# Three column blocks of parameters are issued at a later place of the list schedule

## The chip, the cores and the metric

The kernel runs on one core of one Trainium2 chip. The metric is the time of one execution on the device in microseconds (us), lower is better. TensorE is called PE below, VectorE DVE, ScalarE ACT, SyncE SP (it issues most DMAs), GpSimd POOL.

## The reference, cut to what matters

A decoder trunk of two layers on 512 tokens of width 1024. The first layer mixes tokens with a gated DeltaNet, the second with sliding window attention, and each ends in a gated MLP with a causal depthwise convolution. The change lies in the DeltaNet layer. What is computed there, and the parameters that the change touches:

```python
proj = rmsnorm(h, a_norm_w) @ a_w_in          # q, k, v, z, b, a
qkv = silu(causal_dwconv(qkv, a_conv_w))
q = l2norm(q) * 128 ** -0.5; k = l2norm(k)
o = chunked_gated_delta_rule(q, k, v, g, beta)  # chunks, triangular solve, scan
o = rmsnorm(o, a_out_norm_w) * silu(z)
h = h + o @ a_w_out
...
u = causal_dwconv(rmsnorm(h, ffn_norm_w) @ ffn_w_up, ffn_conv_w, ffn_conv_b)
h = h + (silu(gate) * val) @ ffn_w_down
...
return rmsnorm(h, final_norm_w)
```

The three blocks hold `ffn_conv_w` of both layers (128 rows of each in a block of its own, the four rows left of each in the first block), `a_out_norm_w` and `final_norm_w`. Each is first used long after the place where it is made: `a_out_norm_w` in the gating of the first finished heads, the convolution weights in the first MLP, the last norm at the very end.

## The kernel before, in words

**Dense products.** Every projection is computed in tiles of 128 output columns by 512 tokens. A float32 product is split into three passes (`mm3`: high by high, low by high, high by low), so one tile of a projection from 1024 inputs is 24 PE instructions of shape 128x512, called dense products here (lines L162, L163, L164). They collect in one of three PSUM banks with the tag "d". The weights arrive by SP in stages of 256 columns (`load_stage`, two buffers), and `cast` splits them on ACT (L132) and DVE (L133).

**What follows a tile.** `conv_silu` reads the bank: one ACT step (L277), three DVE steps (L280) and a silu on ACT (L281). It works in a row with the tag "acc" (two buffers) and writes, for values, a row "va" (two buffers). A bank "d" is free once the three DVE steps are done.

**Heads in four groups.** For each group of heads the words of `ORDER` name jobs: K and Q, key and query projections; V, value projections; B, key norms (`key_norms`, L433 to L455); P, key products (`key_products`, L464 to L482, with exponentials on ACT, L475); T, A and R, turned keys (L519), query products (L508, L511) and query norms (L500); I, a triangular solve on DVE (62 short steps, L555 and L561); L, block steps that finish the inverse (`levels`, L585 to L615); C, the scan over four chunks (L635 to L682); z and g, the gate projections and the gating of a finished head. Nearly all of the short PE steps collect in one of only two banks with the tag "g", which ACT or DVE must empty before the next but one step can write.

**What sets the order.** The program is written as one sequence, and a list scheduler puts the instructions of each engine into a fixed order by priority and by when it expects operands and buffers. Each job gets a priority by its place: `base + 1000 * (100 + pos + SHIFT[letter])`, a lower number first. B has a shift of -28, so the key norms come early although their word stands second; V2 and V3 of the first group stand at 118 and 119. What is written before the loop, like the columns, has an earlier priority than all jobs. At run time an engine works its row strictly in order. The buffers of a tag, on the other hand, are handed out in the order in which the program is written.

**Columns.** `columns` loads rows of parameters into a row (for the three blocks the tag "f", by SP), turns them on PE with the identity (L235) into a bank "g", and copies the bank to a constant on DVE (L237). Before the change the three blocks are written after the gates of the DeltaNet and ahead of the loop over `ORDER`.

Of the kernel before, what the change touches and what calls it, by code (L numbers as in the profile page):

```python
# [17 lines left out]
P = 128  # L18
# [17 lines left out]
]  # L36

SHIFT = {"R": 6, "B": -28, "g": -40, "K": -1, "N": 7, "C": -2, "P": -3}


@with_exitstack
def kernel(
# [64 lines left out]
    def row(tag, dt=F32, n=T):  # L107
        return main.tile([P, n], dt, tag=tag, bufs=ROWS[tag], name=nm(tag))
# [4 lines left out]
    def bank(tag):  # L113
        return psum.tile([P, T], F32, tag=tag, bufs=BANKS[tag], name=nm(tag))

    def const(shape, dt=F32, s="c"):
        return cp.tile(list(shape), dt, name=nm(s))
# [109 lines left out]
    def columns(parts, n, s, q=SP, tag="acc", place="g"):  # L227
        st = row(tag, n=P)
        r = 0
        for ap in parts:  # L230
            k = ap.shape[0]
            q.dma_start(st[r : r + k, :], ap)
            r += k
        ps = bank(place)
        PE.transpose(ps[:, :n], st[:n, :], ident[:n, :n])  # L235
        t = const([P, n], s=s)
        V.tensor_copy(t[:], ps[:, :n])  # L237
        return t
# [16 lines left out]
    for c in range(NC):  # L255
        junk = main.tile([P, D], F32, tag="nt", bufs=2, name=nm("junk"))
        r = const([P, 1], s="rx")
# [5 lines left out]
    for k in range(KD):  # L263
# [3 lines left out]
        h, l = row("xh", F32R), row("xl", F32R)  # L267
# [68 lines left out]
    for c in range(NC):  # L336
# [25 lines left out]
        base=0,  # L362
# [13 lines left out]
    def hc(ap):  # L376
# [32 lines left out]
    zd = dp.tile([HV, P, T], F32, name="zd")  # L409
    yd = dp.tile([HV, P, T], F32, name="yd")  # L410

    fconv_rows = ffn_conv_w.rearrange("l j (r c) -> l (j r) c", c=P)
    onw_c = columns(
        [
            fconv_rows[0, 128:132, :],
            fconv_rows[1, 128:132, :],
            a_out_norm_w,
            final_norm_w.rearrange("(r c) -> r c", c=P),
        ],
        17,  # L420
        "onwc",
        tag="f",
    )
    fcw = [columns([fconv_rows[l, 0:128, :]], 128, "fcw", tag="f") for l in range(2)]

    def key_norms(g):
        pr = slice(2 * g, 2 * g + 2)
        st[g]["kk"] = pair("m32")
        for i in range(2):
            kT = st[g]["k"][:, i, :]  # L430
            ps = bank("g")
            cut = [slice(c * P, (c + 1) * P) for c in range(NC)]
            together([lambda cs=cs: PE.matmul(ps[:, cs], kT[:, cs], kT[:, cs], start=True, stop=True) for cs in cut])  # L433
            S.copy(st[g]["kk"][:, i, :], ps[:])
            diag = row("va")
            d3 = diag[:].rearrange("p (c t) -> p c t", c=NC)
            V.tensor_tensor(
                d3,
                ps[:].rearrange("p (c t) -> p c t", c=NC),
                ident[:].unsqueeze(1).to_broadcast([P, NC, P]),  # L440
                op=ALU.mult,
            )
            V.tensor_reduce(sse[:, 0, 2 * g + i, :], d3, axis=AX.X, op=ALU.add)
        V.tensor_scalar(sse[:, 0, pr, :], sse[:, 0, pr, :], EPS, None, op0=ALU.add)
        V.reciprocal(rk2[:, pr, :], sse[:, 0, pr, :])
        S.activation(nk[:, pr, :], sse[:, 0, pr, :], AF.Sqrt)
        for i in range(2):
            hs = slice(4 * g + 2 * i, 4 * g + 2 * i + 2)
            V.tensor_tensor(
                brk[:, hs, :],  # L450
                beta_t[:, hs, :],
                rk2[:, 2 * g + i : 2 * g + i + 1, :].to_broadcast([P, 2, NC]),
                op=ALU.mult,
            )
            V.tensor_tensor(kap[:, hs, :], brk[:, hs, :], egd[:, hs, :], op=ALU.mult)  # L455
# [308 lines left out]
    heads = {"z": 0, "g": 0}  # L764
    base = tc.cur_priority
    pos = 0
    for i, line in enumerate(ORDER):
        for word in line.split():
            a, n = word[0], [int(d) for d in word[1:]]
            pos += 1  # L770
            target = base + 1000 * (100 + pos + SHIFT.get(a, 0))
            with tc.high_priority(tc.cur_priority - target):
                if a in heads:
                    (gate_proj if a == "z" else gate)(heads[a])
                    heads[a] += 1
                elif a.isupper():
                    JOBS[a](i, *n)
                else:
                    JOBS[a.upper()](i - 1, *n)
# [664 lines left out]
```

## Time and profile before

| | |
|---|---|
| time, median of 3 runs | 1415.96 us (1414.63 to 1419.01) |
| span of the profiled execution | 1412.6 us; its own time beyond the span is not recorded |
| PE, PEld, DVE, ACT busy | 98%, 83%, 78%, 53% of the span |
| granted PE clock | 0.999 over the span |
| DeltaNet layer up to its last scan and gates | about the first 450 us |
| three column transposes on PE | 42.6 to 45.9 us |
| first key norms on PE | 46.9 us |
| first `levels` of group 0 on PE | 126.6 us |

The page lists the busy time of each engine and the costliest groups of instructions; the view of the waits says for each instruction what ended the idle time ahead of it; the timeline lists instructions by start and duration, merged where equal ones follow each other (a number after x counts them). PE instructions overlap, so that a dense product that lasts 0.39 us is followed by the next after some 0.23 us. A float32 product appears twice or more in the timeline's count for one row of the program.

### The profile page before, as it was taken

What the parts mean: (1) busy time and instruction counts of PE and PEld (TensorE: products, weight loads), DVE (VectorE), ACT (ScalarE), POOL (GpSimd) and SP (SyncE); (2) the same over time, 40 slices, a digit from 0 to 9 for tenths busy, and PEclk for the clock granted to TensorE, in tenths of its full rate; (3) what the DMA queues carried; (4) which work ended last, traced back from release to release, by engine and by line L of the source; (5) the groups of instructions that cost most, each with busy time, mean ns of one, the idle gap of its engine ahead of it and who ended that gap; (6) DMA issues with size and microseconds to landing.
All of it is one profiled execution on the core that took longest, in us unless ns stands there. A gap on an engine that the chain in (4) does not pass through costs nothing.

```text
span 1412.6 us, 21751 instructions
## 1 busy us (share of the span) xinstructions
PE 1384.7 (98%) x8370; PEld 1167.1 (83%) x8370; DVE 1108.1 (78%) x2070; ACT 748.1 (53%) x1470; POOL 15.6 (1%) x37
## 2 busy tenths in 40 slices
PE   7999999999999999999999999999999999999998
PEld 5787888878877888888988889777788888988897
DVE  4996896978856438879878889788668888878996
ACT  7764566656658225444344446567544444444543
POOL 1000000000100000000000000000000000000000
PEclk9999999999999999999999999999999999999999
DMA  5333254172465323221443223322132231432222
GB/s 161 92 103 115 79 175 126 61 231 84 140 225 159 119 90 112 90 90 46 135 150 119 75 79 109 109 71 76 61 112 90 90 101 49 146 106 82 92 75 75
DMA packets 162299, 151.80 MB, mean 107 GB/s; under 512 B 24148, under 2 KB 150677, under 8 KB 162197
## 3 DMA queue, kind: packets, MB, share of 16 engines
q1 hardware_dynamic: 159938, 150.22, 33.2%
q8 instruction: 66, 1.08, 0.3%
q10 hardware_dynamic: 2259, 0.20, 0.1%
q14 instruction: 36, 0.29, 0.1%
HBM read 133.60 MB, written 15.75 MB: 106 GB/s over the span
## 4 chain that ended last, share of the span: by engine, by line
PE 87%; DVE 6%; DMA 2%; ACT 2%; issue 1%; SPq 0%; DVEq 0%; ACTq 0%
PE d L162 20%; PE d L163 20%; PE d L164 20%; PE g L198 2%; DVE wlo L133 2%; PE d L1054 1%; PE d L1207 1%; PE d L1211 1%; PE d L1209 1%; PE d L1052 1%; PE d L1053 1%; PE s L1054 1%; PE s L1052 1%; PE s L1053 1%; PE s L659 1%
## 5 line engine op out<-in xcount | busy, mean ns | idle before, releaser
L162 PE MATMUL d<-xh,whi 128*128 128x512 f32 x1128 | 444.2, 394 | 0.2
L163 PE MATMUL d<-xl,whi 128*128 128x512 f32 x1128 | 444.0, 394 | 0.0
L164 PE MATMUL d<-xh,wlo 128*128 128x512 f32 x1128 | 441.9, 393 | 0.3 <-DVE wlo L156 0.3
L132 ACT CAST whi<-stage 128x1024 fp32r<-128x1024 f32 (+2 forms) x234 | 227.4, 976 | 247.7 <-PE d L163 165.1
L133 DVE TENSOR_TENSOR wlo<-stage,whi 128x1024 fp32r<-128x1024 f32 (+2 forms) x234 | 263.4, 1128 | 70.4 <-ACT whi L132 69.6
L162 PEld LDWEIGHTS d<-xh,whi 128*128 128x128 f32 x1128 | 211.7, 188 | 44.9 <-ACT xh L172 0.5
L164 PEld LDWEIGHTS d<-xh,wlo 128*128 128x128 f32 x1128 | 211.6, 188 | 44.6 <-DVE wlo L156 0.7
L163 PEld LDWEIGHTS d<-xl,whi 128*128 128x128 f32 x1128 | 211.7, 188 | 43.2 <-issue 0.5
L280 DVE SCALAR_TENSOR_TENSOR acc<-d,cwc,acc 128x511 f32<-128x511 f32 (+2 forms) x96 | 70.7, 739 | 8.7 <-ACT acc L277 7.9
L913 DVE TENSOR_TENSOR sz<-d,p6s 128x512 f32<-128x512 f32 x59 | 40.6, 688 | 42.9 <-PE d L164 40.7
L935 ACT ACTIVATE dt<-dt 128x512 f32<-128x512 f32 x44 | 27.8, 631 | 78.3 <-DVE dt L918 78.3
L918 DVE SCALAR_TENSOR_TENSOR dt<-sz,fcw,dt 128x511 f32<-128x511 f32 (+1 forms) x60 | 44.8, 747 | 1.8 <-ACT dt L916 0.9
L918 DVE SCALAR_TENSOR_TENSOR va<-sz,fcw,va 128x511 f32<-128x511 f32 (+1 forms) x58 | 43.3, 747 | 0.9
L561 DVE TENSOR_TENSOR sT<-sT,p6s 64x31 f32<-64x31 f32 (+15 forms) x124 | 40.9, 330 | 2.0
L555 DVE TENSOR_TENSOR p6s<-sN,sT 64x31 f32<-64x31 f32 (+15 forms) x124 | 40.7, 328 | 1.9
L1276 ACT ACTIVATE dt<-dt,sm 128x256 f32<-128x256 f32 (+1 forms) x64 | 30.1, 471 | 21.5 <-DVE sm L1259 21.5
L132 ACT CAST whi<-st 128x768 fp32r<-128x768 f32 (+1 forms) x30 | 23.7, 792 | 30.5 <-PE g L1053 9.0
L913 DVE TENSOR_TENSOR zl<-d,p6s 128x512 f32<-128x512 f32 x29 | 20.0, 688 | 17.8 <-PE d L164 17.8
L682 ACT ACTIVATE rq<-o 128x128 f32<-128x128 f32 x64 | 19.0, 301 | 25.4 <-DVE o L677 22.3
L937 DVE TENSOR_TENSOR va<-dt,va 128x512 f32<-128x512 f32 x44 | 30.4, 690 | 1.2
L133 DVE TENSOR_TENSOR wlo<-st,whi 128x768 fp32r<-128x768 f32 (+1 forms) x30 | 26.8, 899 | 2.2 <-ACT whi L132 2.2
L916 ACT ACTIVATE dt<-sz,normc,fcw 128x512 f32<-128x512 f32 x30 | 24.5, 815 | 6.5 <-DVE sz L913 6.0
(770 smaller groups left out, 2876.2 us busy)
## 6 DMA issues: line engine op xcount, KB each, us to landing
stage<-in_ffn_w_up_dram SPq DMA_DIRECT2D x44, 1024.0 KB, 4.8
stage<-in_a_w_in_dram SPq DMA_DIRECT2D x23, 1024.0 KB, 5.8
stage<-in_ffn_w_down_dram SPq DMA_DIRECT2D x16, 768.0 KB, 4.3
stage<-in_a_w_out_dram SPq DMA_DIRECT2D x8, 1024.0 KB, 5.0
st<-in_ffn_w_down_dram SPq DMA_DIRECT2D x8, 768.0 KB, 5.3
zd<-sz SPq DMA_DIRECT2D x16, 256.0 KB, 2.6
od<-o SPq DMA_DIRECT2D x16, 256.0 KB
stage<-in_b_w_q_dram SPq DMA_DIRECT2D x4, 1024.0 KB, 5.0
```

The lines of the kernel that those rows point to most:

```text
L132: S.copy(hi[:, :kt, :m], src)
L133: V.tensor_tensor(lo[:, :kt, :m], src, hi[:, :kt, :m].bitcast(F32), op=ALU.subtract)
L162: PE.matmul(ps, hi[:, k, :m], xh[k], start=first and k == 0, stop=False)
L163: PE.matmul(ps, hi[:, k, :m], xl[k][:], start=False, stop=False)
L164: done.append(PE.matmul(ps, lo[:, k, :m], xh[k], start=False, stop=last and k == kt - 1))
L280: V.scalar_tensor_tensor(acc[:, d:], ps[:, : T - d], col, acc[:, d:], op0=ALU.mult, op1=ALU.add)
L555: V.tensor_tensor(tv, N[:, s, s + 1 : 32].unsqueeze(2).to_broadcast([64, n, m]), Tm[:, s : s + 1, 0:m].to_broadcast([64, n, m]), op=ALU.mult,)
L561: V.tensor_tensor(Tm[:, s + 1 : 32, 0:m], Tm[:, s + 1 : 32, 0:m], tv, op=ALU.subtract)
L913: V.tensor_tensor(u[:], ps[:], rs[:], op=ALU.mult)
L918: V.scalar_tensor_tensor(acc[:, d:], u[:, : T - d], tap(2 - d, t), acc[:, d:], op0=ALU.mult, op1=ALU.add)
L937: V.tensor_tensor(b[:], a[:], b[:], op=ALU.mult)
L1276: S.activation(ej, ej, AF.Exp, bias=ngm[:, i : i + 1], scale=-1.0, accum_out=den[:, i : i + 1])
```

## The change

The code that makes the three blocks moves behind the definitions of all jobs, directly ahead of the loop over `ORDER`, and gets a priority of its own, that of a job at place 20: behind V2 and V3 of the first group (118 and 119), and ahead of most of the second line of `ORDER`. Nothing else changes; the same DMAs, transposes and copies are issued.

```diff
+COLUMNS = 20
 SHIFT = {"R": 6, "B": -28, "g": -40, "K": -1, "N": 7, "C": -2, "P": -3}
...
-    fconv_rows = ffn_conv_w.rearrange("l j (r c) -> l (j r) c", c=P)
-    onw_c = columns(
...
-    fcw = [columns([fconv_rows[l, 0:128, :]], 128, "fcw", tag="f") for l in range(2)]
...
     base = tc.cur_priority
     pos = 0
+    with tc.high_priority(tc.cur_priority - base - 1000 * (100 + COLUMNS)):
+        fconv_rows = ffn_conv_w.rearrange("l j (r c) -> l (j r) c", c=P)
+        onw_c = columns(
+            [
+                fconv_rows[0, 128:132, :],
+                fconv_rows[1, 128:132, :],
+                a_out_norm_w,
+                final_norm_w.rearrange("(r c) -> r c", c=P),
+            ],
+            17,
+            "onwc",
+            tag="f",
+        )
+        fcw = [columns([fconv_rows[l, 0:128, :]], 128, "fcw", tag="f") for l in range(2)]
     for i, line in enumerate(ORDER):
```

The line numbers of the changed program are one higher up to the old place of the block and 13 lower between the two places (L433 becomes L420, L464 becomes L451, L508 becomes L495, L605 becomes L592). The numbers at the end of names tell buffers apart in the order of the program.

**First place, PE, the columns and the first key norms, before.** These rows follow the turned gates; the names are g_365, g_371, g_377 for the columns and g_420 for the first key norms, and d_634 is the first query tile.

```order
L235 MATMUL g_365<-ident_81,f_360 128x17
L162 MATMUL d_634<-xh_178,whi_635 128x512
L163 MATMUL d_634<-xl_179,whi_635 128x512
L164 MATMUL d_634<-xh_178,wlo_636 128x512
L162 MATMUL d_634<-xh_187,whi_635 128x512
L235 MATMUL g_371<-ident_81,f_369 128x128
L235 MATMUL g_377<-ident_81,f_375 128x128
L163 MATMUL d_634<-xl_188,whi_635 128x512
L164 MATMUL d_634<-xh_187,wlo_636 128x512
L162 MATMUL d_634<-xh_196,whi_635 128x512
L163 MATMUL d_634<-xl_197,whi_635 128x512
L433 MATMUL g_420<-kT_206 128x128 x4
```

The same place in the changed program. Here d_843 is the tile of the value head V3, and d_1186 the first key tile of the second group of heads.

```order
L165 MATMUL d_843<-xh_196,wlo_845 128x512
L236 MATMUL g_368<-ident_81,f_363 128x17
L236 MATMUL g_374<-ident_81,f_372 128x128
L163 MATMUL d_1186<-xh_133,whi_1187 128x512
L236 MATMUL g_380<-ident_81,f_378 128x128
L164 MATMUL d_1186<-xl_134,whi_1187 128x512
L420 MATMUL g_420<-kT_206 128x128 x4
L420 MATMUL g_429<-kT_206 128x128 x4
L165 MATMUL d_1186<-xh_133,wlo_1188 128x512
```

Counted along PE's row, 87 dense products stand ahead of the first column transpose before, and 192 in the changed program. The key norms have moved with the columns, from behind 95 dense products to behind 194: they stand after the columns in both, and their banks are numbered after those of the columns.

**Second place, PE, the short steps of the first group.** Before, they are spread between dense products; around the first value transpose (g_579) and the first turned keys (g_623) PE's row reads as follows, where d_721 is the tile of V1.

```order
L162 MATMUL d_721<-xh_178,whi_722 128x512
L198 MATMUL g_579<-ident_81,va_540 128x128 x4
L198 MATMUL g_623<-ident_81,kT_206 128x128 x4
L163 MATMUL d_721<-xl_179,whi_722 128x512
L164 MATMUL d_721<-xh_178,wlo_723 128x512
```

In the changed program the third and fourth key product (g_475, g_489), the value transposes of V0 and V1 (from va_540, va_720), the turned keys, two query products and two query transposes stand in one piece.

```order
L451 MATMUL g_475<-gr_301,skr_315 128x512
L452 MATMUL g_475<-mnegr_322,identr_86 128x512
L451 MATMUL g_489<-gr_301,skr_315 128x512
L452 MATMUL g_489<-mnegr_322,identr_86 128x512
L199 MATMUL g_579<-ident_81,va_540 128x128 x4
L199 MATMUL g_623<-ident_81,kT_206 128x128 x4
L495 MATMUL g_704<-qT_631,kT_206 128x128 x4
L495 MATMUL g_712<-qT_631,kT_206 128x128 x4
L199 MATMUL g_756<-ident_81,va_720 128x128 x4
L199 MATMUL g_765<-ident_81,qT_631 128x128 x4
L199 MATMUL g_775<-ident_81,qT_631 128x128 x4
L199 MATMUL g_786<-ident_81,kT_206 128x128 x4
```

Ahead of this piece lies dense product 216, the last of d_1186, and behind it comes d_1221; between the two no dense product is left. ACT's row for the same stretch in the changed program (dt are the exponentials of the key products, nk the root of the key norms, va the silu of V0 and V1):

```order
L462 ACT_TABLE_LOAD
L462 ACTIVATE dt_449<-g_446,ngc_331 128x128
L433 ACT_TABLE_LOAD
L433 ACTIVATE nk_351<-sse_350 128x8
L462 ACT_TABLE_LOAD
L462 ACTIVATE dt_449<-g_446,ngc_331 128x128 x3
L462 ACTIVATE dt_463<-g_460,ngc_331 128x128 x4
L462 ACTIVATE dt_478<-g_475,ngc_331 128x128 x4
L462 ACTIVATE dt_492<-g_489,ngc_331 128x128 x4
L282 ACT_TABLE_LOAD
L282 ACTIVATE va_540<-acc_572 128x512
L282 ACTIVATE va_720<-acc_750 128x512
```

Before, too, the table loads and the 16 exponentials stand ahead of the silu of V0 on ACT; what has moved is that PE now has its row of short steps, and no dense product, beside them.

**Third place, PE, the end of the fourth group's `levels`.** Before, dense products of the last gate projection (d_4404) stand between its steps; p_4050 and s_4061 are its last two block steps, s_4133 is the first product of the scan.

```order
L162 MATMUL d_4404<-xh_160,whi_4405 128x512
L163 MATMUL d_4404<-xl_161,whi_4405 128x512
L164 MATMUL d_4404<-xh_160,wlo_4406 128x512
L605 MATMUL p_4050<-Xg,nt_3418 64x64 x8
L162 MATMUL d_4404<-xh_169,whi_4405 128x512
L163 MATMUL d_4404<-xl_170,whi_4405 128x512
L164 MATMUL d_4404<-xh_169,wlo_4406 128x512
L612 MATMUL s_4061<-sy_4001,p6s_347 64x64 x8
L651 MATMUL s_4133<-vt_3773,sy_3929 128x128 x2
```

In the changed program, where d_4625 and d_4683 are the first tiles of the output projection:

```order
L581 MATMUL s_4022<-sy_4001,pz_346 32x32
L592 MATMUL p_4050<-Xg,nt_3418 64x64 x8
L599 MATMUL s_4061<-sy_4001,p6s_347 64x64 x8
L638 MATMUL s_4133<-vt_3773,sy_3929 128x128 x2
L163 MATMUL d_4625<-kT_4478,whi_4626 128x512
L163 MATMUL d_4683<-kT_4478,whi_4684 128x512
L638 MATMUL s_4133<-vt_3866,sy_4001 128x128 x2
```

All 1152 dense products of the layer's input projections are issued ahead of these steps now. From the first half's middle step (s_3950) to s_4133, 17 dense products stand between the steps before, and none now. In the scan behind, four dense products stand now between the second chunk's two pieces (L638 and L646), where none stood before (L651 and L659), and one instead of four between the same pieces of the first chunk.

More of the change, by code (lines that the diff above doesn't have):

```diff
@@ L410 @@
     yd = dp.tile([HV, P, T], F32, name="yd")
-    fconv_rows = ffn_conv_w.rearrange("l j (r c) -> l (j r) c", c=P)
-    onw_c = columns(
[L414 to L423, printed above, removed]
-    fcw = [columns([fconv_rows[l, 0:128, :]], 128, "fcw", tag="f") for l in range(2)]
     def key_norms(g):
```

## The prediction

> **What bounds the kernel now.** I read the page's busy times first, then the waits of PE up to 520 us, then the timeline where the change works.
>
> ```profile
> span 1412.6 us, 21751 instructions
> PE 1384.7 (98%) x8370; PEld 1167.1 (83%) x8370; DVE 1108.1 (78%) x2070; ACT 748.1 (53%) x1470; POOL 15.6 (1%) x37
> ```
>
> PE is busy for 98% of the span, so a wait of PE that comes or goes moves the end by its length, unless a later one absorbs it. How much there is to win the waits tell (engine, line, what it waited for: us in total, times, longest):
>
> ```profile
> PE g L235 <- DMA xt<-in_x_dram: 8.4, 1, 8.4
> PE g L235 <- DVE onwc L237: 1.7, 1, 1.7
> PE p L659 <- ACT us L653: 1.5, 1, 1.5
> PE g L198 <- ACT ol L720: 1.0, 1, 1.0
> PE s L266 <- DVE xt L261: 0.7, 1, 0.7
> PE d L162 <- ACT kT L168: 0.5, 1, 0.5
> ```
>
> Behind the start-up there are four waits in 520 us, 4.7 us together. One belongs to the columns. The next rows give it and the pace of the dense products:
>
> ```profile
> 27.89 0.40 PE L162 MATMUL d<-xh,whi 128*128 128x512 f32 x1
> ...
> 42.00 0.39 PE L164 MATMUL d<-xh,wlo 128*128 128x512 f32 x1
> 42.23 0.44 PE L370 MATMUL g<-ident,sz 80*128 80x80 f32 x4
> ...
> 45.41 0.17 DVE L237 COPY onwc<-g 128x17 f32<-128x17 f32 x1
> ...
> 45.63 0.48 PE L235 MATMUL g<-ident,f 128*128 128x128 f32 x2 [1.68 <-DVE onwc L237]
> ```
>
> From 27.89 to 42.00 lie 63 dense products: (42.00 - 27.89) / 62 = 0.2276 us each. The second column transpose needs the bank of the first, whose copy waited in DVE's queue until 45.41.
>
> **The change, step by step.** No work is added or removed; PE's row is permuted, and the question is what PE waits for in the new row. I write T for the time since PE reaches the first column transpose there.
>
> *The old wait goes: -1.7.* At the new place DVE stands empty before the copies, since the last convolution ahead of them belongs to the tile V1, two tiles back. Three copies of the kind above then cost PE some 0.3 us. T = 0 lies at 42.7 + 105 x 0.2276 = 66.6 us, 105 dense products behind the turned gates. Until there nothing should wait: a tile takes 24 x 0.2276 = 5.5 us of PE and, by the next rows, about 3 x 0.73 + 1.21 = 3.4 us of DVE.
>
> *The new piece without dense products.* The key norms did not pass the columns but were pulled back with them, behind 99 more dense products. V0 to V3 cannot finish before them: two hold the two rows "acc", and V2, V3 and the next key tile fill the three banks "d". So PE runs out of dense products at number 216, and works the piece of ten short groups alone. The rows that price it:
>
> ```profile
> 43.62 1.21 DVE L133 TENSOR_TENSOR wlo<-stage,whi 128x1024 fp32r<-128x1024 f32 x1
> ...
> 46.88 2.00 PE L433 MATMUL g<-kT 128*128 128x128 f32 x16
> 48.03 0.59 ACT L434 COPY m<-g 128x512 f32<-128x512 f32 x1 [0.32 <-PE g L433]
> 48.65 0.69 DVE L437 TENSOR_TENSOR va<-g,ident 128x512 f32<-128x512 f32 x1 [0.43 <-ACT m L434]
> 49.49 0.46 PE L464 MATMUL g<-gr,skr 128*128 128x512 f32 x1
> ...
> 53.23 1.28 ACT L446 ACT_TABLE_LOAD   x1
> ...
> 56.03 2.18 ACT L475 ACTIVATE dt<-g,ngc 128x128 f32<-128x128 f32 x8
> 58.22 1.28 ACT L281 ACT_TABLE_LOAD   x1
> 59.52 0.63 ACT L281 ACTIVATE va<-acc 128x512 f32<-128x512 f32 x1
> 60.22 0.64 PE L198 MATMUL g<-ident,va 128*128 128x128 f32 x4
> ...
> 61.15 1.14 ACT L538 ACTIVATE vt<-g,nk 128x128 f32<-128x128 f32 x4
> ...
> 61.94 1.28 DVE L519 TENSOR_TENSOR ktok<-g,kap 128x512 f32<-128x512 f32 x2
> ...
> 63.14 2.89 DVE L280 SCALAR_TENSOR_TENSOR acc<-d,cwc,acc 128x510 f32<-128x510 f32 x4
> 63.24 0.69 ACT L277 ACTIVATE acc<-d,cwc 128x512 f32<-128x512 f32 x1
> ...
> 66.39 1.95 PE L508 MATMUL g<-qT,kT 128*128 128x128 f32 x16
> ...
> 67.73 2.47 DVE L511 TENSOR_TENSOR at<-g,dt 128x512 f32<-128x512 f32 x4
> ...
> 70.12 0.17 DVE L555 TENSOR_TENSOR p6s<-sN,sT 64x31 f32<-64x31 f32 x1
> ...
> 77.67 0.27 ACT L500 ACTIVATE va<-g 128x128 f32<-128x128 f32 x1
> ```
>
> PE reaches the piece at T = 9.4: 24 dense products 5.5, columns 0.6, key norms 2.0, two key products 0.6 each. ACT meanwhile: the norms start at T = 1.2, the second copy (0.59, from 48.03) is over at 3.8; then a table load 1.28, one exponential 0.27, a load, the root 0.2, a load, and the other seven exponentials 1.9: T = 10.2, when the fourth key product gets its bank. PE ends it at 10.9. Then eight exponentials 2.2, a load 1.3 and the silu 0.63 end at 14.3 on ACT; the transpose of V0 needs it, so PE is idle for 3.5. The turned keys follow to 15.3. A query product needs the bank of V0, which ACT empties (1.14) behind a second silu and a convolution step (1.2): 16.7, idle 1.4. Two query products (1.95) end at 18.6. V1's transpose waits for the first of them to be read: DVE does ktok (1.28), two convolution steps (1.45) and two of the four at (1.24) by 19.5, idle 0.9; the first query transpose waits for the other two, 20.8, idle 0.8; the second for ACT's copies of V1, 0.1; the last turned keys for four squares with their sums (about 1.2 from 77.67 on), 22.6, idle 0.8. PE leaves the piece at T = 23.0. Of these 13.6 us its own work is 1.3 + 0.9 + 1.95 + 1.8 = 5.9. **Wait: 7.7.** Behind it two value transposes and the next key norms wait some 0.2 to 0.3 each for silus that come late: with the columns' 0.3, **0.9**.
>
> Bounds: at least the 3.5 for V0 and half of the rest, 5.5, were the chain behind it to overlap better than I draw it; at most 11, with 0.4 more at each of eight hand-overs (the end of the silu at 60.15 to 60.22 in the rows shows 0.1).
>
> [...]
>
> *Group 0 comes later: 0, between 0 and 3.* Its solve starts on DVE (70.12 now) at about T = 25.7, 92.3 us. Its `levels` stand behind 419 dense products instead of 385, at 66.6 + 23.0 + 203 x 0.2276 + about 7 for short steps = 142.8. So 50.5 us are left between them, where now it is 56.4:
>
> ```profile
> 126.55 0.24 PE L585 MATMUL s<-Xg,nt 32*32 32x32 f32 x2
> ```
>
> Yet DVE has three convolution steps and two weight splits less in between (3 x 0.73 + 2 x 1.21 = 4.6), so I take nothing. The 16 DMAs of the key products wait on SP behind two weight stages more; these load before the products exist. If the cover is gone, PE waits 1 to 3 us here.
>
> *The end of the layer: +2.1.* The 17 dense products between the fourth group's `levels` steps are gone, and its chain through DVE and ACT stays:
>
> ```profile
> 405.38 0.50 PE L162 MATMUL d<-xh,whi 128*128 128x512 f32 x1
> 405.51 0.42 DVE L596 TENSOR_SCALAR Xg<-s 32x256 f32<-32x256 f32 x1 [1.36 <-PE s L594]
> 406.28 0.68 PE L605 MATMUL p<-Xg,nt 64*64 64x64 f32 x16
> ...
> 407.06 0.76 ACT L608 COPY p6s<-p 64x256 f32<-64x256 f32 x2 [2.58 <-PE p L605]
> 407.78 0.76 PE L612 MATMUL s<-sy,p6s 64*64 64x64 f32 x16
> ```
>
> Each step starts 0.1 to 0.4 behind the one it needs, so the chain is no shorter without the dense products, and PE waits for their 17 x 0.2276 = 3.9. In the scan the 1.5 (L659) and 0.5 (L162) of the waits go, as four dense products stand there now; the first chunk's copy (0.6 with 0.3 of hand-over) has one dense product instead of four and costs 0.65. Now three dense products from 405.38 end at 406.06 and the next step starts at 406.28, so 0.2 is waited for already; I take the same for the other half. Sum 3.9 + 0.65 - 1.5 - 0.5 - 0.4 = 2.1. Bounds -2 (nothing of the 3.9 seen) and +5.
>
> **Sum:** -1.7 + 7.7 + 0.9 + 0 + 2.1 = +9.0. The profiled span of 1412.6 becomes 1421.6. The three timed runs lie 2.0 to 6.4 above that span, the median 3.4; I add the sum to the median: 1416.0 + 9.0 = 1425.0.
>
> **Rivals.** *The wait is hidden.* The piece is fed faster than I draw, the layer's end loses nothing, and only the columns' wait goes: 1416.0 - 1.7 = 1414.3. For it: now PE passes the same steps without a wait. Against: now 93 dense products stand among these ten groups (between numbers 106 and 199), and then none.
>
> *Faster.* Convolutions and casts run ahead by 24 us, and the scan's end finds its operands ready: 1.7 + 1.5 + 0.5 + 1.0 (L198) = 4.7 go, 1411.3. This decides only if the ten groups wait under 1 us in all, while two banks and the exponentials already demand 3.5 for V0 alone.
>
> *A slower PE clock.* The array was slower after its idle start:
>
> ```profile
> 13.54 0.80 PE L162 MATMUL d<-xh,whi 128*128 128x512 f32 x1
> ...
> 19.95 0.39 PE L164 MATMUL d<-xh,wlo 128*128 128x512 f32 x1
> ```
>
> The same product took 0.80 and later 0.39. If the 13.6 us of thin work bring this back, the 5.9 us in them double at most, of which about half lies on the chain, and the dense products behind lose 1 to 2: +4, 1429. [...] Late `levels` of group 0 (+1 to +3) end in the same place.
>
> *The change does what it says,* with the columns behind the key products: 1414.3 as well. The key norms' banks are numbered behind the columns', and their rows stand behind them, so it has no chance of its own.
>
> **How the numbers follow.** Forecast 1425, own range 1420.3 to 1428, chance 0.55. Slower clock or late `levels`, about 1429, 0.25. Wait hidden, about 1414 to 1420, 0.17. Faster, 0.03. A measurement of this kernel can tell about 0.3%, 4.2 us, from no change: slower 0.80, same 0.17, faster 0.03. The range takes in the low bound of the piece with a gain at the end (-1.7 + 5.5 + 0.3 - 2 = +2) and the high one (-1.7 + 11 + 0.9 + 5 = +15): 1417.5 to 1431.
>
> **What the profile would show.** Right: no wait at L236 above 0.5; the key norms near 68 us; PE waiting 6 to 9 us between about 76 and 90, first 3 to 4 us for ACT's silu of V0, then for DVE's at and ACT's squares; waits of 3 to 4 us in the fourth group's `levels`. Wrong: waits under 3 us in the piece, a first `levels` of group 0 that waits, or dense products of 0.8 behind it.

## The result, and the profile after

| | before | after |
|---|---|---|
| time, median of 6 runs each, taken together | 1417.78 us (1414.63 to 1419.52) | 1429.88 us (1428.56 to 1432.95) |
| ratio to before, 95% interval | | 1.0094 (1.0080 to 1.0107) |
| profiled execution: time, span | not recorded, 1412.6 us | 1429.34 us, 1427.5 us |
| granted PE clock over the span | 0.999 | 0.994 |

The change makes the kernel slower by 12.1 us (the difference of the medians). The forecast was 9.0 us and a time of 1425.0; of the 4.9 us between this and 1429.88, 1.8 is the base, whose median moved from 1415.96 to 1417.78 with three more runs. The two profiles are executions with a clock at the upper end of what their kernels show: 0.999, where the 61 executions of the kernel before in the sets of the experiments have 0.995 to 0.999, and 0.994, where the change's other five have 0.992 and 0.993. Line numbers of the changed kernel are used from here on: L163 to L165 dense products, L199 turns, L236 columns, L420 key norms, L451 and L452 key products, L495 query products, L579 to L599 `levels`, L638 and L646 the scan.

The page's head and its busy times, after:

```profile
span 1427.5 us, 21769 instructions
PE 1391.6 (97%) x8370; PEld 1171.3 (82%) x8370; DVE 1109.5 (78%) x2070; ACT 748.9 (52%) x1471; POOL 12.6 (1%) x37
```

PE executes the same 8370 instructions and is busy 6.9 us longer. So only about half of the 14.9 us that the span grew is idle time; the rest is slower work. The waits of PE up to 490 us (instruction, what it waited for, us in total, times, longest; the first is the start-up, and smaller ones follow):

```profile
PE g L236 <- DMA acc<-in_ffn_conv_b_dram: 7.8, 1, 7.8
PE g L199 <- ACT va L282: 3.3, 1, 3.3
PE g L199 <- ACT ol L707: 1.4, 3, 0.7
PE p L592 <- DVE Xg L583: 1.1, 2, 0.5
PE g L199 <- DVE at L498: 1.0, 1, 1.0
PE s L599 <- ACT p6s L595: 1.0, 2, 0.5
PE d L163 <- ACT at L169: 0.9, 1, 0.9
PE s L579 <- ACT pz L575: 0.8, 1, 0.8
PE g L199 <- ACT va L487: 0.8, 1, 0.8
...
```

The columns' wait of 1.7 is gone. V0's turn waits 3.3 for its silu, the forecast's largest single wait. Waits of about 0.5 stand ahead of the fourth group's `levels` steps. The timeline of PE in the early stretch (start, us, line, tiles, shape, count, idle before it and what ended it):

```profile
65.85 2.02 PE L420 MATMUL g<-kT 128*128 128x128 f32 x16
...
78.95 1.12 PE L199 MATMUL g<-ident,va 128*128 128x128 f32 x4 [3.29 <-ACT va L282]
79.86 1.06 PE L199 MATMUL g<-ident,kT 128*128 128x128 f32 x4
81.30 3.77 PE L495 MATMUL g<-qT,kT 128*128 128x128 f32 x16 [0.38 <-ACT vt L525]
84.90 0.63 PE L199 MATMUL g<-ident,va 128*128 128x128 f32 x4
86.54 1.06 PE L199 MATMUL g<-ident,qT 128*128 128x128 f32 x8 [1.00 <-DVE at L498]
88.40 0.66 PE L199 MATMUL g<-ident,kT 128*128 128x128 f32 x4 [0.79 <-ACT va L487]
88.81 0.48 PE L163 MATMUL d<-xh,whi 128*128 128x512 f32 x1
```

The key norms stand at 65.85, 19 us later than before. Behind the long wait the same turn takes 1.12 and then, at 84.90, 0.63, and the query products take 3.77 where they took 1.95 before. The view by stretches says why (us, busy PE, PEld, DVE, ACT and POOL with their instructions, granted clock, DMA share, GB/s). Before, in two windows, one of each stretch:

```profile
80.00:85.00 5.00, 5.00 (x27) 4.10 (x27) 4.90 (x14) 3.44 (x12) 0.00 (x0) 1.00 0.05 17
405.00:410.00 5.00, 5.00 (x93) 3.94 (x83) 2.64 (x6) 1.87 (x4) 0.30 (x1) 1.00 0.54 172
```

After:

```profile
80.00:85.00 5.00, 4.62 (x22) 4.13 (x21) 3.80 (x6) 2.65 (x6) 0.00 (x0) 0.51 0.17 26
85.00:90.00 5.00, 3.20 (x22) 2.46 (x22) 4.82 (x9) 3.94 (x22) 0.00 (x0) 1.00 0.17 56
420.00:425.00 5.00, 3.96 (x43) 3.45 (x38) 4.30 (x8) 2.49 (x5) 0.30 (x1) 0.50 0.38 129
```

The clock was halved in the early stretch (0.51) and again at the layer's end (0.50), where in the profile of before it was 1.00 in every such window. The second pair of the last `levels` steps, after:

```profile
420.62 1.12 PE L592 MATMUL p<-Xg,nt 64*64 64x64 f32 x16 [0.52 <-DVE Xg L583]
422.26 1.50 PE L599 MATMUL s<-sy,p6s 64*64 64x64 f32 x16 [0.52 <-ACT p6s L595]
423.69 1.22 PE L638 MATMUL s<-vt,sy 128*128 128x128 f32 x4
```

The same steps took 0.68 and 0.76 before. **To count both losses** I read windows of 1 us from 36 to 490 us, and take as idle the part in which PE isn't busy, and as slow its busy part times (1 - clock). Two of these rows, after:

```profile
79.00:80.00 1.00, 1.00 (x5) 1.00 (x6) 0.05 (x1) 0.99 (x2) 0.00 (x0) 0.50 0.22 34
420.00:421.00 1.00, 0.48 (x13) 0.38 (x8) 0.82 (x2) 1.00 (x2) 0.00 (x0) 0.50 0.21 70
```

The first adds 0.50 to slow and nothing to idle, the second 0.24 to slow and 0.52 to idle. The sums of 454 rows:

| us, idle / slow | 36-60 | 60-110 | 110-400 | 400-440 | 440-490 | all |
|---|---|---|---|---|---|---|
| before | 1.67 / 0 | 0.04 / 0 | 1.18 / 0 | 1.99 / 0 | 0.09 / 0 | 4.97 / 0 |
| after | 0 / 0 | 5.75 / 2.79 | 2.03 / 0 | 3.77 / 2.81 | 1.24 / 0 | 12.79 / 5.60 |

That is 7.8 more idle and 5.6 slow, 13.4 together, beside 14.9 in the spans and 12.1 in the medians. The 0 of slow before holds for the profiled execution alone: of those 61 executions, the 13 with a clock of 0.999 took 1415.2 on average and the 9 with 0.996 took 1419.6, so most executions of the kernel before lose some time to the clock too, at a place that no kept trace shows.

Last, the stores of the four groups' solves (line, count, ns, first and last start), before, and then after:

```profile
L564 SPq DMA_DIRECT2D td<-sT x4: 471/494/655, 119.4 to 381.0; - x4
```

```profile
L551 SPq DMA_DIRECT2D td<-sT x4: 474/492/498, 132.6 to 396.2; - x4
```

The first solve ends 13.2 later and the fourth 15.2 later: the lateness of the key norms is handed from group to group. PE's dense products are late by less (by 8.0 at the 1151st, counted with the gates' 24: 406.96 instead of 398.94), and in PE's fixed row all of them stand ahead of the fourth group's last `levels` steps now.

### The profile page after: what moved, and what is told of

The parts are those of the page before. It is cut to its first block, busy times and chain, and to the rows that moved or that the text cites. A ratio compares the mean times of both kernels' runs of the same rounds, so it can differ in the third digit from the quotient of the medians.

```text
span 1427.5 us, 21769 instructions
## 1 busy us (share of the span) xinstructions
PE 1391.6 (97%) x8370; PEld 1171.3 (82%) x8370; DVE 1109.5 (78%) x2070; ACT 748.9 (52%) x1471; POOL 12.6 (1%) x37
## 4 chain that ended last, share of the span: by engine, by line
PE 85%; DVE 6%; DMA 4%; ACT 3%; issue 1%; DVEq 0%; SPq 0%; ACTq 0%
PE d L163 19%; PE d L165 19%; PE d L164 19%; PE g L199 2%; DVE wlo L134 2%; DMA ol<-od 1%; PE d L1208 1%; PE d L1212 1%; PE d L1210 1%; PE d L1055 1%; PE s L638 1%; PE d L1053 1%; PE d L1054 1%; PE s L1055 1%; PE s L646 1%
## 5 line engine op out<-in xcount | busy, mean ns | idle before, releaser
L165 PE MATMUL d<-xh,wlo 128*128 128x512 f32 x1128 | 444.3, 395 | 1.2 <-DVE wlo L134 0.9
L163 PE MATMUL d<-xh,whi 128*128 128x512 f32 x1128 | 444.3, 394 | 0.2
L165 PEld LDWEIGHTS d<-xh,wlo 128*128 128x128 f32 x1128 | 211.6, 188 | 46.4 <-DVE wlo L134 1.9
L163 PEld LDWEIGHTS d<-xh,whi 128*128 128x128 f32 x1128 | 211.8, 188 | 44.1 <-issue 0.6
```

Of the source, the lines that this page charges most:

```text
L163: PE.matmul(ps, hi[:, k, :m], xh[k], start=first and k == 0, stop=False)
L165: done.append(PE.matmul(ps, lo[:, k, :m], xh[k], start=False, stop=last and k == kt - 1))
```

## The experiments

Each kernel is compared with the kernel before, run in the same set on the same chip. The column "all" is the sum of idle and slow of that kernel's profile, and of the work without use that it adds, less the 4.97 of before; the last column is the difference of the medians in its set.

| run | median us | ratio, 95% interval | idle | slow | added | all | medians |
|---|---|---|---|---|---|---|---|
| 1 other banks | 1419.04 | 1.0013 (1.0000 to 1.0027) | 6.80 | 1.71 | | +3.5 | +2.2 |
| 2 one late | 1431.51 | 1.0095 (1.0077 to 1.0113) | 13.49 | 5.77 | | +14.3 | +14.7 |
| 3 norms late alone | 1431.87 | 1.0100 (1.0078 to 1.0122) | 15.07 | 5.63 | | +15.7 | +15.2 |
| 4 COLUMNS 16 | 1427.43 | 1.0065 (1.0048 to 1.0083) | 11.98 | 5.81 | | +12.8 | +10.6 |
| 5 end alone | 1424.52 | 1.0062 (1.0041 to 1.0082) | 7.63 | 6.88 | | +9.5 | +8.7 |
| 6 end undone | 1441.05 | 1.0168 (1.0146 to 1.0189) | 16.16 | 15.30 | | +26.5 | +25.2 |
| 7 early filled | 1429.35 | 1.0080 (1.0063 to 1.0097) | 10.06 | 4.42 | 3.2 | +12.7 | +12.5 |
| 8 end filled, first try | 1433.96 | 1.0124 (1.0105 to 1.0143) | 11.63 | 7.52 | 1.8 | +16.0 | +18.2 |
| 9 end filled, half width | 1432.04 | 1.0102 (1.0085 to 1.0118) | 10.61 | 7.71 | 2.6 | +16.0 | +15.4 |
| 10 both, half width at the end | 1432.40 | 1.0110 (1.0094 to 1.0125) | 8.17 | 6.65 | 5.8 | +15.7 | +15.8 |
| 11 end filled, full width | 1427.30 | 1.0071 (1.0056 to 1.0086) | 9.33 | 2.49 | 3.6 | +10.5 | +9.2 |
| 12 both, full width | 1426.74 | 1.0069 (1.0049 to 1.0090) | 8.38 | 3.41 | 6.8 | +13.6 | +9.4 |
| 13 norms five products later | 1417.97 | 1.0012 (0.9996 to 1.0028) | 6.10 | 0 | | +1.1 | +2.2 |

The two last columns agree within 2.3 us in every row but the twelfth, from 1 to 26 us. The sums are those of one execution each, the medians of 4 to 17. So what a version costs is read on PE, as waits plus slow clock.

### What holds the work back: runs 1 to 3

**1, other banks.** The late transposes write to another tag:

```diff
-            tag="f",
-        )
-        fcw = [columns([fconv_rows[l, 0:128, :]], 128, "fcw", tag="f") for l in range(2)]
+            tag="f",
+            place="s",
+        )
+        fcw = [columns([fconv_rows[l, 0:128, :]], 128, "fcw", tag="f", place="s") for l in range(2)]
```

> The three late transposes write to the two PSUM banks of tag s instead of the two of tag g; nothing else differs from the change. The transposes then still stand behind dense product 192, but the key norms stand behind 87, as before, and the ten short groups have dense products among them again; the layer's end has the order of before. Theory A (what costs is the order in which tag g hands out its banks: it holds back the key norms and empties two stretches of dense products): no wait of PE over 1.0 us between 75 and 95, granted clock 1.00 in the 5 us windows from 75 to 90 and from 415 to 430, and a time of 1416 (1414 to 1418), at or 1.7 under the kernel before. Rival B (the late place of the transposes, their copies and their loads costs by itself): a time within 2 us of the change, 1428 to 1432.

Measured 1419.04, 2.2 over the kernel before (interval 0 to 0.27%), and no wait or slow clock between 60 and 110. Rival B (1428 to 1432) falls. Theory A has the mechanism; the time is 1 us above its range, and in the profile another wait stands in the place of the columns' wait. PE of this kernel:

```profile
43.84 0.47 PE L163 MATMUL d<-xh,whi 128*128 128x512 f32 x1
46.23 1.18 PE L420 MATMUL g<-kT 128*128 128x128 f32 x8 [1.92 <-ACT gt L375]
47.15 0.70 PE L164 MATMUL d<-xl,whi 128*128 128x512 f32 x1
47.64 0.63 PE L165 MATMUL d<-xh,wlo 128*128 128x512 f32 x1
...
50.62 0.41 PE L163 MATMUL d<-xh,whi 128*128 128x512 f32 x1
```

The second key norms need the bank of the turned gates and wait 1.92 for ACT's copy of it. Behind that, dense products start 0.43 apart instead of 0.23 up to 50.6: the clock was halved here too (0.50 in every half microsecond from 47.5 to 50.5).

**2, one late.** Only the second `fcw` gets the later place, the rest stands as before.

```diff
+    fcw = [columns([fconv_rows[0, 0:128, :]], 128, "fcw", tag="f")]
...
+        fcw.append(columns([fconv_rows[1, 0:128, :]], 128, "fcw", tag="f"))
```

> Only the second block of 128 rows (the second fcw) has the later place; the other two stand where they stood before. Theory A: a single late block holds back the bank as three do; PE's order between dense products 192 and 216 and in the layer's end is that of the change, so 1430 (1428 to 1432), with two clock windows near 0.5. Rival B (the cost goes with the number of late blocks): a third of the 12 us, 1422 (1420 to 1424).

Measured 1431.51, as theory A has it. The cost does not go with the number of late blocks: one in the ring of tag g is enough.

**3, norms late alone.** The kernel before, its columns at their old place, with one tie:

```diff
+    behind(st[0]["norms", 0], passes[HQK * P + 256][0])
```

> The kernel before with its three blocks of columns at their old place, and one tie: the first group's first key norms stand behind the first dense products of the second group's key projection (number 195). PE's order from there on, the piece of ten short groups and the layer's end, is that of the change. Theory A (what costs is the key norms that are held back; the columns are only what holds them in the change): as the change and a columns' wait of 1.7 more, 1431.5 (1429 to 1433.5), clock 0.5 for some microseconds near 80 and near 420. Rival B (the late columns, their loads and copies cost a part): under 1427.

Measured 1431.87, at theory A's 1431.5, with the columns' wait back (1.82 idle from 36 to 60) and the clock down in both stretches (0.50 in the half microseconds from 81.5 to 84.5, 0.50 from 420 to 425). With run 1 this settles who is to blame: late columns with early key norms cost 2.2, early columns with late key norms 15.2.

### The two stretches apart: runs 4 to 6

**4, COLUMNS 16.**

```diff
-COLUMNS = 20
+COLUMNS = 16
```

> COLUMNS is 16 instead of 20: the transposes stand behind dense product 144, the key norms behind 146, and the ten short groups have dense products among them up to number 211; the layer's end has the order of the change, with all 1152 dense products of the projections issued before the fourth group's last levels steps. Theory A (two drained stretches with costs of their own, +7.3 early and +5.9 at the layer's end): the early stretch costs -1.7 to +1.5, the layer's end +5.9 again, about +1 behind it, so 1424 (1421 to 1427); clock 1.00 from 75 to 90 and about 0.5 from 420 to 425. Rival B (the loss at the layer's end follows from the late early stretch): clock 1.00 at the layer's end and a time of 1417 to 1420.

Measured 1427.43, just above theory A's range, and rival B (1417 to 1420) falls: from 60 to 110 PE idles 0.4 and the clock stays (1.00 in the three windows of 5 us from 75 to 90), and the layer's end still idles 3.4 and loses 4.1. What theory A missed is the middle, 5.0 idle and 1.7 slow from 110 to 400, the first of it here:

```profile
135.78 0.22 PE L572 MATMUL s<-Xg,nt 32*32 32x32 f32 x2 [0.68 <-DMA Xg<-td]
137.15 0.87 PE L199 MATMUL g<-ident,va 128*128 128x128 f32 x4 [1.16 <-ACT va L282]
```

Here the first `levels` of group 0 waits for its solve. Its solves' stores, the view of the result's last two fences:

```profile
L551 SPq DMA_DIRECT2D td<-sT x4: 471/492/499, 126.8 to 393.9; - x4
```

They are late too (7.4 and 12.9 us), though PE lost nothing early. Time that PE does not lose early it loses where the late solves are needed.

**5, end alone.** The kernel before, with one tie that puts the fourth group's first step behind the projections' last dense product:

```diff
+    behind(st[3]["step"][0], passes[QKV + 256 * 7 + P][-1])
```

> The kernel before, its columns at their old place, with one tie added: the fourth group's first levels step with pz stands behind the last dense product of the projections, as in the change. Nothing of the early stretch differs from before. Theory A: the layer's end alone costs +5.9 over the kernel before, 1422.7 (1421 to 1424.5), with clock 0.5 for some 6 us between 410 and 430 and waits of about 0.5 at each step. Rival B (the loss needs the early delay too): 1416 to 1418.5.

Measured 1424.52, at the upper end of theory A's range: the emptied layer's end costs 8.7 on its own. It is no exact copy of the change's end. The clock was low for 17.1 us (407.5 to 424.6) instead of 6.8, and one wait in it is longer:

```profile
409.47 0.47 PE L614 MATMUL s<-sy,p6s 64*64 64x64 f32 x2 [3.21 <-ACT p6s L609]
```

ACT made that copy only at 409.05, behind a weight cast that waited for its DMA until 407.98. The bound is therefore rough.

**6, end undone.** The change, its last 24 dense products of the projections tied behind the steps:

```diff
+BEHIND = (7, 15, 15, 23, 31, 31, 39, 39)
...
+    s3 = st[3]["step"]
+    for k, at in enumerate(BEHIND):
+        behind(starts[QKV + 256 * 7 + P][k], s3[at])
```

> The change, with the last 24 dense products of the projections tied behind the fourth group's levels steps, three to a step at most places, so that the layer's end has dense products among its steps as the kernel before has; the early stretch, with its ten short groups in one piece, stays as the change has it. Theory A (the layer's end costs +5.9, because its steps lost the dense products that covered their waits and kept the clock up): clock 1.00 from 415 to 430, still 0.5 in 80 to 85, and a time of 1424 (1422.5 to 1425.5). Rival B (the layer's end is late for another reason, its loads or ACT's and DVE's work): 1428 to 1431, with the waits at other instructions.

A miss: 1441.05, beyond both. The moved products were missing ahead of the steps, where they had covered ACT's and DVE's work (waits of 1.97 at 412.75 for ACT's `ol` and 1.96 at 416.90 for DVE's `sy`), the clock fell at 413.8, and did not come back for 24 us:

```profile
425.00:430.00 5.00, 5.00 (x56) 2.96 (x55) 2.12 (x4) 1.06 (x2) 0.00 (x0) 0.50 0.50 157
430.00:435.00 5.00, 5.00 (x41) 3.90 (x41) 1.20 (x3) 0.73 (x2) 0.30 (x1) 0.50 0.01 3
```

In this order group 0's first `levels` also waited for its solve (2.1 at L580), and 1.6 were lost to the clock there, as in run 4. So this order does not give the cover back: what is put between the steps is missing ahead of them. That the steps lost their cover stays the reading of the trace and of run 5, not of this run.

### What the clock costs: runs 7 to 12

All of these are the change with products without use (the mask by the identity) added to keep the array working. **7** puts 14 ahead of V0's transposes:

```diff
+            if (g, hh) == (0, 3):
+                fill = bank("p")
+                st[0]["fill"] = [
+                    PE.matmul(
+                        fill[:].rearrange("p (c t) -> p c t", c=NC),
+                        identr[:],
+                        mnegr[:].unsqueeze(1).to_broadcast([P, NC, P]),
...
+                    for _ in range(FILL)
+                ]
+                behind(st[0]["fill"][0], bias)
```

> The change, plus 14 products of 128x512 without use (the mask by the identity, into the bank of tag p that nothing reads then) between the last key product of the first group and V0's transposes, 14 x 0.2276 = 3.2 us of work in the 3.3 us in which PE waits for silu of V0. Everything else stands in the same order. Theory A (the 3.3 us of idle lower the clock, and the lower clock lies on PE's path through the short groups): clock 1.00 from 75 to 90, the 16 query products 1.95 instead of 3.77, dense products resume 1.5 to 3 us earlier, time 1427.5 (1426 to 1428.5). Rival C (the short groups are fed by ACT and DVE, and PE's clock there is hidden): clock 1.00, but longer waits in place of the slower products, and a time of 1429 to 1431.

The clock stayed, 1.00:

```profile
80.00:85.00 5.00, 3.06 (x25) 2.55 (x23) 4.46 (x8) 2.99 (x7) 0.00 (x0) 1.00 0.18 29
```

The query products took 2.05, but the waits behind them grew (1.03, 0.91, 0.56 and 0.54 at the four that follow), and the median is 1429.35, rival C's. Counted at the 311th dense product of each trace, less the offset at the 7th (the start differs by up to 2 us between runs), the change is 7.3 later than before and this kernel 6.2. The other profiles in which the early stretch is as the change has it give 7.1 to 7.3 (runs 6, 8, 9 and 11), the one of run 12, where the clock stayed as well, 6.1, and that of run 10, where it fell in spite of the added work, 7.1. Of the early loss about 1.1 is the clock; the rest of the 2.8 is hidden behind ACT and DVE. The median does not show the 1.1, since it holds the layer's end as well, where this profile lost 4.4 to the clock and that of the change 2.8.

**8** puts four products of 128x256 behind each of four steps at the layer's end, into the bank that the step has written:

```diff
+FILLED = ((3, 0, 3), (3, 0, 6), (3, 0, 7), (3, 1, 1))
...
+        def fill(ps, step):
+            for _ in range(KEEP if (g, pr, step) in FILLED else 0):
...
+        fill(p3, 3)
```

> The change, plus 16 products of 128x256 without use (four into the unused half of each of four banks of the fourth group's levels steps), 16 x 0.114 = 1.8 us of work, in waits of PE of about 0.5 each. Theory A (of the +5.9 at the layer's end some 3.4 is the lower clock and 2.5 waits): clock 1.00 from 415 to 430, the steps back at their lengths of before (0.76 instead of 1.50), time 1427 (1425.5 to 1428.5). Rival C (as in the early stretch, where a full clock took 1.1 off 7.3, the waits grow by what the steps shrink): clock 1.00 and a time of 1429 to 1430.5.

A miss of the design, 1433.96: waits of about 0.5, and one of 1.2, stood behind the added products as they had stood without them; my reading, not tested by itself, is that the copies that PE waits for read the bank that these products still wrote. The clock fell later, at 423.8, and stayed down for 10.2 us. It tells nothing about the clock's price.

**9** puts them ahead of each waiting step, in the half of that step's bank that it does not use:

```diff
+KEEP = {(3, 0, 6): 4, (3, 0, 7): 4, (3, 1, 3): 7, (3, 1, 6): 4, (3, 1, 7): 4}
...
+        fill(p3, 3)
         for c in range(8):
```

> The change, plus 23 products of 128x256 without use at the layer's end (23 x 0.114 = 2.6 us), this time ahead of each waiting step, in the unused half of the bank that this step writes itself, so that no copy waits for them. Added over windows of 1 us, PE of the change is idle 3.8 us and loses 2.8 us to the lower clock between 400 and 440. Theory A (the lower clock is on PE's path there): clock 1.00 from 400 to 440, idle below 2.5, and a time 2 to 4 us under the change, 1426 to 1428. Rival C (ACT and DVE set the pace of these steps, PE's clock is hidden): the steps end when they ended before, and the time is 1429 to 1431.

Idle fell to 1.3, and the clock still went to 0.5 at 420.4, so that 1432.04 is neither theory's case. **10** is this with the 14 products of run 7:

> The change with both sets of products without use, 14 of 128x512 ahead of V0's transposes and 23 of 128x256 at the layer's end. Theory A (without the lower clock the change costs what the prediction's other terms say): clock 1.00 in every window from 36 to 490, and 1424 to 1427. Rival C: clock 1.00 and 1429 to 1431.

Measured 1432.40, with the clock down in both stretches (1.6 and 5.0 slow): again it was not kept, and nothing follows on its price.

**11** has 16 products of full width, in a bank that this step or the one behind it overwrites:

```diff
+KEEP = {(3, 0, 6): 3, (3, 0, 7): 3, (3, 1, 3): 4, (3, 1, 6): 3, (3, 1, 7): 3}
...
+                    ps[:].rearrange("p (c t) -> p c t", c=NC),
...
+        p6 = bank("p")
+        fill(p6, 3)
```

> The change, plus 16 products of 128x512 without use at the layer's end (three or four ahead of each of the five waiting steps, 16 x 0.2276 = 3.6 us, in a bank that the step itself overwrites later), where the run before this one had 23 of 128x256 and the clock still fell at 420. Theory A (PE needs full products between the thin steps to keep its clock, and the lower clock is on its path): clock 1.00 from 408 to 440, the second pair's steps at 0.7 to 0.8 instead of 1.1 to 1.5, idle and slow clock together under 1 instead of 6.6, so the end 2 to 3.5 us earlier for 3.6 us of added work, 1426 to 1428.5. Rival C (ACT's and DVE's copies set the pace): clock 1.00, and 1429 to 1431. Rival E (full products don't keep the clock either): clock 0.5 near 420, and 1431 to 1434.

Measured 1427.30, in theory A's range. The stretch in run 9, and then in run 11:

```profile
420.00:425.00 5.00, 5.00 (x77) 4.37 (x78) 4.22 (x7) 2.83 (x5) 0.30 (x1) 0.54 0.52 175
```

```profile
415.00:420.00 5.00, 5.00 (x118) 3.55 (x120) 1.98 (x6) 2.18 (x5) 0.30 (x1) 1.00 1.02 358
420.00:425.00 5.00, 4.89 (x70) 3.55 (x61) 4.70 (x9) 2.92 (x6) 0.31 (x1) 1.00 0.44 125
```

With the clock kept, PE gets 3.6 us of useless work done and the kernel is still faster: the ratio to before falls from 1.0094 to 1.0071 (the intervals, 1.0080 to 1.0107 and 1.0056 to 1.0086, just overlap). Idle and slow from 400 to 440 are 0.65 instead of 6.58, so 5.9 are saved for 3.6 spent. The added work stands where 3.1 of waits were and costs 0.5 beyond them; the 2.8 of slow clock is what more than pays for it. At the layer's end the lower clock is on PE's path.

**12** joins runs 7 and 11:

> The change with both sets of full products without use that kept the clock up one at a time: 14 of 128x512 ahead of V0's transposes (3.2 us of work) and 16 of 128x512 at the layer's end (3.6 us). Theory A (the prediction's terms hold for waits, and its miss is the lower clock in both stretches): clock 1.00 in every window from 36 to 490, idle over that stretch about 7 plus 6.8 of added work against 12.8 idle and 5.6 slow in the change, so 3 to 5 us under the change, 1425 to 1427. Rival C (early, the clock is hidden behind ACT and DVE, so the second set adds nothing to the first): as the run with the layer's end alone, 1427 to 1428.5.

Measured 1426.74, in theory A's range, but only 0.6 under run 11, and against the kernel before in its own set no gain at all (9.4 over it, run 11 9.2), which is what rival C says: the early set pays for itself at most. Its profiled execution is the slowest of its six (1429.68, mean clock 0.996): a pause of 0.6 at 420.35 was followed by a halved clock from 422.6 to 429.4. The other five had 0.999.

### A version nearly without the loss: run 13

Run 1 with the second key norms five dense products later, so that less of the wait for the gates is idle:

```diff
+    behind(st[0]["norms", 1], passes[0][6])
```

> The late transposes in the banks of tag s, as in the first experiment, and the second key norms of the first group behind dense product 93 instead of 88; nothing else differs from the first experiment. There PE waited 1.92 for ACT's copy of the gates, and the eight dense products behind that wait took 0.43 each instead of 0.23. Five more dense products ahead of the wait take 1.1 of it: if that keeps the clock up (theory A), the wait is 0.8, no dense product takes over 0.30 near 47, and the time is 2 to 3 us under the first experiment, 1415 to 1417, level with the kernel before within 0.3%. Rival D (the wait only moves, or the products of the next steps wait in its place): 1418 to 1420.

Measured 1417.97 against 1415.81, ratio 1.0012 (0.9996 to 1.0028). In the profile the wait for the gates is 0.73, the clock stayed at 1.00 up to 490, and waits of 0.95 and 0.40 stand at the next key products, so that PE idles no less than in run 1 there. That execution is one of the two with a clock of 0.999; four of the twelve have 0.995 or 0.996 and took 1421.8 to 1423.8. The median is 1 us above the range of theory A and at the edge of rival D's, and the two are not told apart. No version run here is faster than the kernel before.

## Why the prediction was off, point by point

**The columns' wait, -1.7: right for the change.** From 36 to 60 PE does not idle. But it was no gain in itself: with the key norms in time (run 1) the gates' copy is waited for instead.

**The order of bank g as the cause: right, and shown** by runs 1 to 3.

**The early piece, +7.7 + 0.9 - 1.7 = +6.9: right in sum, by luck.** Idle and slow from 36 to 110 rose by 4.0 + 2.8 = 6.8. The make-up differs: V0's wait was 3.3 (forecast 3.5), but all waits were 5.75 instead of 7.7 + 0.9 = 8.6, and slower products, which the sum left out, took up the rest. ACT and DVE caught up under them: with the clock kept (run 7) part of that time turns into waits again (1.03 instead of 0.38 ahead of the query products, 0.91 instead of none ahead of the turn behind them).

**Group 0's late `levels`, 0: right for PE in the change.** They start at 140.9 (forecast 142.8) without a wait, and 110 to 400 idles 0.85 more. What I did not follow further is that the solves end 13 to 15 us late in all groups; in run 4 this lateness was waited for in the middle instead.

**The layer's end, +2.1: the waits were right, and the clock was missing.** Idle from 400 to 440 rose by 1.8: 2.9 in the `levels` (forecast 3.9 - 0.4), 0.4 for the first chunk's copy (0.65), 0.45 for `ol` (in no term), and the 1.5 and 0.5 of the scan are gone. The 0.4 was misread: before, the third of the dense products from 405.38 lasts until 406.35, so PE waits for nothing at 406.28. The 2.8 of slow clock beside it were in no term, and 1.15 of waits behind the scan (0.9 of it at L163, for ACT's copy `at`) neither.

**The step that failed** is the one that set the slower clock aside. The prediction had it as a rival with a chance of 0.25 and one place, the early piece, for +4. It happened, and in two places, 5.6 in the profile, and at the layer's end it made the term of +2.1 into 4.6. Run 11 shows what it did to the time: with the clock kept there, 9.2 over before is left. That this is close to the forecast's 9.0 says little, as useless work fills part of the waits by then. The forecast counted idle time and took every instruction at its length of before. In the early stretch, with its gap of 3.29, and at the end, with nothing but products of 32x32 and 64x64 in the steps, such lengths did not hold: 1.95 became 3.77 and 0.76 became 1.50. The price given to the early clock was too high (about 1.1 lies on the path, not 4); the place where it does cost was the layer's end. So it is luck that the rival's 1429 lies near the measured 1429.9.

**The range.** The bounds that the prediction adds up for it, 1417.5 to 1431 (the lower one is 1418 by its own terms), hold the measured time. The range that it states, 1420.3 to 1428, does not take them in, though the text reads as if it did.

**What was to be seen in the profile** was mostly seen: no wait at L236, the key norms near 68 (65.85), waits between 76 and 90 (5.5 in the rows above where 6 to 9 were named), and 2.9 in the last `levels` (three rows of the waits, where 3 to 4 were named). The sign named for a slower clock, dense products of 0.8 behind the piece, could not come: the clock was low from 78.1 to 84.9, while PE worked the short groups, and the first dense product behind them, at 88.81, took 0.48.

## What to carry to other kernels

A buffer ring is handed out in the order of the program, so moving one user late moves every later user of that ring with it; before giving work a later place, look at what stands behind it in the ring rather than at the work itself. When a change takes dense products out from between small ones, ask not only which waits open but whether the clock will hold, and price the small products at twice their length if it may not (here 1.50 instead of 0.76). And a lateness that is free where it begins is followed to the next place where covering work runs out.

## What the runs showed of the hardware

**In these runs the lower clock, 0.50, came in pieces of 3.4 us.** In windows of half a microsecond it lasted from about 47.2 to 50.6 (run 1), 137.5 to 140.9 (run 4), 78.1 to 84.9 and 419.4 to 426.3 in the change, 420.4 to 430.7 (run 9), 407.5 to 424.6 (run 5), and 413.8 to 437.7 in run 6: 1, 1, 2, 2, 3, 5 and 7 times 3.4.

**It fell behind pauses shorter than one piece.** It fell 2.4 us into a pause (at 78.1, the last key product having ended at 75.7), behind a pause of 1.92 (run 1) but not behind 1.68 (before), and in run 9 at 420.4, behind a pause of only 0.83 with PE else busy:

```profile
415.00:420.00 5.00, 4.17 (x115) 3.51 (x104) 2.28 (x6) 2.07 (x6) 0.30 (x1) 1.00 1.02 337
```

**PE's busy share did not tell whether it came back.** In run 6 PE was busy 5.00 of 5.00 us in the windows from 420 to 435, with dense products between products of 32x32 and 64x64, and the clock stayed at 0.50; in the kernel before a like mix ran at 1.00 (the window from 405 to 410). In run 1 it was back at 1.00 behind eight dense products in a row, from 51.0 on. What it goes by, and which work is enough to keep it, was not settled: with 16 full products it was 1.00 from 415 to 425 in run 11 and, by their mean clock of 0.999, stayed up in five of six executions of run 12, and with 23 of half width it fell (0.54 from 420 to 425 in run 9).
